# Padding so that the tiles TensorE reads begin on a multiple of 128 bytes in SBUF

## The chip, the cores and the metric

The kernel runs on one core of a Trainium2 chip. The metric is the device time of one execution in microseconds (us). Lower is better. The on-chip memory from which the engines read is SBUF: 128 partitions, each a row of bytes. A tile is a block of bytes at the same address in every partition, and "address" below always means the byte address inside a partition. TensorE (PE in the profile) reads two tiles for each matmul: the stationary one (the weights, loaded ahead by a weight load, PEld) and the moving one, which it streams past the weights. VectorE is DVE, ScalarE is ACT.

## The reference

One layer of an encoder for 1024 tokens of width 1024, all in float32:

```python
h = x + 0.5 * swiglu_ffn(rmsnorm(x, norm_ffn1), ffn1_w_in, ffn1_w_out)      # D_FF = 2816
proj = rmsnorm(h, norm_mix) @ w_in                                         # q, k, v, g_ret, p, gates
ret = rmsnorm_per_head(retention(rotary(q), rotary(k) / 16, v)) * silu(g_ret)
pool_out = multiscale_pool(p, pool_w, pool_scale)
gate = sigmoid(gates + gate_bias)
merged = gate[0] * (ret @ w_ret_up) + gate[1] * (pool_out @ w_pool_up)
h = h + merged @ w_out
h = h + 0.5 * swiglu_ffn(rmsnorm(h, norm_ffn2), ffn2_w_in, ffn2_w_out)
out = rmsnorm(h, norm_final)
```

## The kernel before, in words

Every large product is done in three matmuls with float32r operands (`mm3`, lines 171 to 173): each operand tile holds a high part and a low part side by side, written by ACT (`copy`, L151) and DVE (`tt`, L152) in `split`, and the product is high x high + high x low + low x high. Most products are 128x128 weights against 512 moving columns. In the common parts of pairs of groups (`common`) and in the retention stage they have 256 moving columns. The seven-product scheme in `strassen`, `pairs_of_both` and `ffn_out` makes further operand tiles from sums and differences, which is DVE's work.

The stages run one after the other: the first feed-forward block's input products (names `a_...`), its output products (`b...`), the projections, retention with pooling, the merge, and the second feed-forward block (`c_...`, `d...`). `Flow` sets the order: each step prepares its weights four steps ahead, and between steps one or two pieces of deferred DVE and ACT work are issued. The order of instructions is fixed when the program is built.

**Where tiles lie.** Tiles come from two pools in SBUF, `cp` (constants, kept throughout) and behind it `sb`. In a pool, each tag has its own buffers, tags follow each other in the order of their first use, and each buffer takes its size, rounded up to 32 bytes. The tiles of `cp` take 256 (`vec`), 256 (`neg`), 1344 (`cst`), 32 (`warm`), 1024 (`zero`) and 512 (`ones_r`) bytes, from address 1152 on, so `sb` begins at 4576, which is 96 bytes past a multiple of 128. In `sb` the order is: 13 buffers of 4096 bytes (tags `t4`, nine, and `raw`, four); the two buffers of `ss`, of 32 bytes each (sums of squares, eight columns, tiles `x_sums`, `ss0` to `ss3` and `n4sse`); 37 buffers of 4096 bytes (tags `mv`, `wt`, `tl`); eight of 2048 (`c2`); then small tiles and `dec`. All slices that matmuls take of a tile begin at multiples of 512 bytes from its start, so the remainder of an address by 128 is that of its tile.

Worked out from the built program's addresses, the 10668 matmuls of the kernel before divide as follows. The offsets are those of the moving and of the stationary tile, in bytes past a multiple of 128.

| moving columns | moving at | stationary at | matmuls | what they are |
|---|---|---|---|---|
| 512 | 32 | 32 | 8028 | nearly all products |
| 512 | 32 | 96 | 14 | `ones_r` as weights |
| 256 | 32 | 32 | 1818 | `common`, retention |
| 256 | 32 | 96 | 144 | retention, weights `sm` (a `t4` buffer) |
| 256 | 96 | 32 | 372 | blocks and `state` kept in `t4` buffers |
| 128 | 32 | 32 | 96 | scores of retention |
| 128 (transposes) | 0 | 32 or 96 | 144 | moving is the identity in `cst` |
| 1 and idle (`zero`) | 0 or 96 | 96 | 52 | token sums, the start |

Of the kernel before, what the change touches and what calls it, by code (L numbers as in the profile page):

```python
# [10 lines left out]
F32 = mybir.dt.float32  # L11
# [6 lines left out]
P = 128  # L18
# [71 lines left out]
def block_kernel(ctx: ExitStack, tc, x, x_tok, vecs, f1_in, f1_out, w_in, w_v, pool_w, w_ret, w_pool, w_o,  # L90
# [10 lines left out]
    cp = ctx.enter_context(tc.tile_pool(name="cp", bufs=1))  # L101
    sb = ctx.enter_context(tc.tile_pool(name="sb", bufs=1))
# [14 lines left out]
    def tl(name):  # L117
        return sb.tile([P, S], F32, tag="tl", bufs=N_TL, name=name)
# [4 lines left out]
    def c2(name):  # L123
        return sb.tile([P, H], F32, tag="c2", bufs=N_C2, name=name)

    def bank(name):
        return ps.tile([P, H], F32, tag="ps", name=name)

    def sum_bank(name):

        return ps.tile([P, H], F32, tag="sum", bufs=N_SUM, name=name)

    def load(dst, src):
        nc.sync.dma_start(dst, src)
# [4 lines left out]
    def half(t, j):  # L139
        return t[:, j * H : (j + 1) * H]  # L140
# [52 lines left out]
            mm(b, zero[:, :P], zero, start=True, stop=True)  # L193
    ident, ones = cst[:, C_ID : C_ID + P], cst[:, C_ONE : C_ONE + P]
    ones_r = cp.tile([P, P], F32R, name="ones_r")


    def inverse_root(sums, n, name):
# [17 lines left out]
    def token_sums(ssq, tiles, name):  # L216

        sums = bank(f"{name}sum")
        for k, j in enumerate(tiles):
            mm(sums[:, k : k + 1], ssq[:, j * P : (j + 1) * P], ones[:, :1], start=k == 0, stop=True,  # L220
               skip_group_check=True)
        return sums[:, : len(tiles)]

    def spread(r, name):

        n = r.shape[-1]
        b = bank(f"{name}b")[:, : n * P]
        r2 = sb.tile([P, 2, 8], F32R, tag="r2", bufs=1, name=f"{name}r2")
        split(r2[:, 0, :n], r2[:, 1, :n], r)
        for z in range(2):  # L230
            dg = sb.tile([P, H], F32R, tag="c2", bufs=N_C2, name=f"{name}dg{z}")[:, : n * P]
            for j in range(n):
                at, by = dg[:, j * P : (j + 1) * P], r2[:, z, j : j + 1].bitcast(F32)
                if z:
                    nc.vector.tensor_scalar(at, ident, by, None, MUL)
                else:
                    act(at, ident, AF.Copy, scale=by)
            mm(b, ones_r, dg, start=not z, stop=bool(z))
        return b
# [175 lines left out]
    def strassen(nx, wa, wb, name, evac, end, begin=None, shared=(), dest=None):  # L415
# [43 lines left out]
        def b1():  # L459
            if begin:  # L460
                begin()
            t["a"] = bank(f"{name}a")
            prod("a", "L11", "R11", True, False)
            t["b"] = sum_bank(f"{name}b")
            with soon():
                copy(t["b"], t["a"])
# [535 lines left out]
    load(cst, consts)  # L1002
    flow.add(lambda: copy(ones_r, ones))
    first.work(first.r11, first.r21, first.r12, first.r22, first.p22, first.t2, first.t3, first.t1, first.t4_)
    x_sums = sb.tile([P, 8], F32, tag="ss", bufs=2, name="x_sums")

    def x_square(t):
        r = tl(f"xs{t}")
# [38 lines left out]
    def await_stored(*names):  # L1047
        flow.until(lambda: stored.issuperset(names))
# [311 lines left out]
    class Unit:  # L1360
# [5 lines left out]
        def loads(self):  # L1366
            await_stored(f"q{self.h}", f"k{self.h}", f"v{self.name}")
            at = slice(self.nh * H, (self.nh + 1) * H)
            self.src = {}
            r = self.src["v"] = tl(f"v{self.name}")  # L1370
            load(r, vs[self.h // 2 * 2 + self.nh][:, self.h % 2 * S : (self.h % 2 + 1) * S])
            for n, spilled in (("q", qs), ("k", ks)):
                r = self.src[n] = tl(f"{n}{self.name}")
                for i in range(2):
                    load(half(r, i), spilled[2 * self.h + i][:, at])
            if self.nh == 0:
                self.dec = sb.tile([P, H], F32, tag="dec", bufs=1, name=f"dec{self.h}")
                load(self.dec, decay[self.h])
                self.ss = sb.tile([P, 8], F32, tag="ss", bufs=2, name=f"ss{self.h}")
                self.O = {}  # L1380

        def follow(self, u):
# [278 lines left out]
    class Last(Norm):  # L1661
# [15 lines left out]
        def turned(self, acc):  # L1677


            def gains():  # L1680
                self.row = sb.tile([P, S], F32, tag="mv", bufs=N_MV, name=f"{self.name}row")
                load(self.row, g_row)
                self.ssq_e = sb.tile([P, 8], F32, tag="ss", bufs=2, name=f"{self.name}sse")

            def done(n):

                o = self.rows[n] = sb.tile([P, S], F32, tag="mv", bufs=N_MV, name=f"{self.name}o{n}")
                b = self.turn([acc[mt] for mt in range(4)], n)
                act(half(o, 1), b, AF.Square, accum_out=self.ssq_e[:, n : n + 1])
                tt(half(o, 0), b, half(self.row, 0), MUL)  # L1690
                v = self.sums[n] = sb.tile([P, 8], F32, tag="st", bufs=10, name=f"{self.name}e{n}")[:, :1]
                nc.vector.tensor_scalar(v, self.ssq_e[:, n : n + 1], 1.0 / D, EPS, MUL, ADD)

            def rest(n):

                b = self.turn([acc[mt] for mt in range(4, 8)], n)
                if n < N_SUM:
                    self.banks[n] = sum_bank(f"{self.name}s{n}")
                    copy(self.banks[n], b)
                else:  # L1700
                    copy(half(self.rows[n], 1), b)

            return gains, *(lambda f=f, n=n: f(n) for n in range(4) for f in (done, rest))
# [144 lines left out]
```

## Time and profile before

| | |
|---|---|
| time, median of 3 runs | 2164.43 us (2164.16 to 2165.67) |
| profiled execution: span from first to last instruction | 2160.9 us (no other time is given for it; the median lies 3.5 us above) |
| PE busy | 2148.0 us (99%), 10668 matmuls |
| PEld busy | 1816.9 us (84%) |
| DVE busy | 1870.0 us (87%) |
| ACT busy | 1088.9 us (50%) |
| granted TensorE clock | 0.999 |
| DMA | 320.92 MB, 149 GB/s over the span |

The busy time of PE is a union of spans that overlap, since matmuls are pipelined: a matmul is shown as 0.39 us long where the next begins after 0.23 us. What a matmul costs in a dense run is therefore read from the distance of starts in the timeline, and not from its own length.

### The profile page before, as it was taken

What the parts mean: (1) busy time and instruction counts of PE and PEld (TensorE: products, weight loads), DVE (VectorE), ACT (ScalarE), POOL (GpSimd) and SP (SyncE); (2) the same over time, 40 slices, a digit from 0 to 9 for tenths busy, and PEclk for the clock granted to TensorE, in tenths of its full rate; (3) what the DMA queues carried; (4) which work ended last, traced back from release to release, by engine and by line L of the source; (5) the groups of instructions that cost most, each with busy time, mean ns of one, the idle gap of its engine ahead of it and who ended that gap; (6) DMA issues with size and microseconds to landing.
All of it is one profiled execution on the core that took longest, in us unless ns stands there. A gap on an engine that the chain in (4) does not pass through costs nothing.

```text
span 2160.9 us, 29697 instructions
## 1 busy us (share of the span) xinstructions
PE 2148.0 (99%) x10668; PEld 1816.9 (84%) x10668; DVE 1870.0 (87%) x3300; ACT 1088.9 (50%) x2047; POOL 0.2 (0%) x4
## 2 busy tenths in 40 slices
PE   9999999999999999999999999999999999999998
PEld 7888888888888888888888898887888888888887
DVE  8799899998788798899767877899999989999784
ACT  8544444545656444444426754446644444455463
POOL 0000000000000000000000000000000000000000
PEclk9999999999999999999999999999999999999999
DMA  7232323596323333333485567624133232359532
GB/s 261 69 129 104 101 93 127 165 339 207 122 93 107 109 127 108 118 107 119 153 268 191 167 224 256 218 97 160 65 117 103 98 107 99 118 185 334 178 122 78
DMA packets 117828, 320.92 MB, mean 149 GB/s; under 512 B 12976, under 2 KB 17200, under 8 KB 117680
## 3 DMA queue, kind: packets, MB, share of 16 engines
q1 hardware_dynamic: 117104, 317.97, 43.4%
q8 instruction: 83, 1.36, 0.3%
q10 hardware_dynamic: 576, 1.05, 0.1%
q14 instruction: 65, 0.53, 0.1%
HBM read 228.27 MB, written 90.70 MB: 148 GB/s over the span
## 4 chain that ended last, share of the span: by engine, by line
PE 90%; DVE 7%; ACT 1%; issue 1%; DMA 1%; SPq 0%; ACTq 0%; DVEq 0%
PE c_b L171 2%; PE c_b L173 2%; PE c_b L172 2%; PE a_b L173 2%; PE a_b L171 2%; PE a_b L172 2%; PE c_e L173 2%; PE c_e L171 2%; PE c_e L172 2%; PE a_e L173 2%; PE a_e L171 1%; PE a_e L172 1%; PE bp6b L172 1%; PE bp6b L173 1%; PE bp6b L171 1%; PE c_a L172 1%
## 5 line engine op out<-in xcount | busy, mean ns | idle before, releaser
L172 PE MATMUL c_b<-n3T,c_wS 128*128 128x512 f32 x176 | 68.5, 389 | 0.0
L173 PE MATMUL c_b<-n3T,c_wS 128*128 128x512 f32 x176 | 68.5, 389 | 0.0
L171 PE MATMUL c_b<-n3T,c_wS 128*128 128x512 f32 x176 | 68.2, 390 | 0.0
L171 PE MATMUL a_b<-n1T,a_wS 128*128 128x512 f32 x168 | 65.5, 390 | 0.0
L172 PE MATMUL a_b<-n1T,a_wS 128*128 128x512 f32 x168 | 65.4, 389 | 0.0
L173 PE MATMUL a_b<-n1T,a_wS 128*128 128x512 f32 x168 | 65.4, 389 | 0.0
L173 PE MATMUL a_a<-n1R,a_wL 128*128 128x512 f32 x120 | 46.7, 390 | 0.8 <-DVE a_wL L152 0.8
L171 PE MATMUL a_a<-n1R,a_wL 128*128 128x512 f32 x120 | 46.8, 390 | 0.0
L172 PE MATMUL a_a<-n1R,a_wL 128*128 128x512 f32 x120 | 46.7, 389 | 0.0
L172 PE MATMUL c_a<-n3R,c_wL 128*128 128x512 f32 x112 | 43.7, 390 | 0.0
L171 PE MATMUL c_a<-n3R,c_wL 128*128 128x512 f32 x112 | 43.6, 389 | 0.0
L173 PE MATMUL c_a<-n3R,c_wL 128*128 128x512 f32 x112 | 43.6, 389 | 0.0
L173 PEld LDWEIGHTS c_b<-n3T,c_wS 128*128 128x128 f32 x176 | 33.0, 188 | 6.9
L171 PEld LDWEIGHTS c_b<-n3T,c_wS 128*128 128x128 f32 x176 | 33.0, 188 | 6.9
L172 PEld LDWEIGHTS c_b<-n3T,c_wS 128*128 128x128 f32 x176 | 33.0, 188 | 6.8
L171 PEld LDWEIGHTS a_b<-n1T,a_wS 128*128 128x128 f32 x168 | 31.5, 188 | 6.8 <-ACT a_v L471 0.3
L173 PEld LDWEIGHTS a_b<-n1T,a_wS 128*128 128x128 f32 x168 | 31.5, 188 | 6.6
L172 PEld LDWEIGHTS a_b<-n1T,a_wS 128*128 128x128 f32 x168 | 31.5, 188 | 6.5
L173 PE MATMUL c_e<-n3T,c_wS 128*128 128x512 f32 x88 | 35.1, 399 | 0.4 <-DVE c_wS L152 0.4
L171 PE MATMUL c_e<-n3T,c_wS 128*128 128x512 f32 x88 | 34.5, 393 | 0.0
L172 PE MATMUL c_e<-n3T,c_wS 128*128 128x512 f32 x88 | 34.4, 391 | 0.0
L173 PE MATMUL a_e<-n1T,a_wS 128*128 128x512 f32 x84 | 33.4, 398 | 0.9 <-DVE a_wS L152 0.9
(3058 smaller groups left out, 8076.2 us busy)
## 6 DMA issues: line engine op xcount, KB each, us to landing
c_ra<-in_f_in SPq DMA_DIRECT2D x22, 512.0 KB, 3.6
c_rb<-in_f_in SPq DMA_DIRECT2D x22, 512.0 KB, 4.1
a_ra<-in_f_in SPq DMA_DIRECT2D x21, 512.0 KB, 3.6
a_rb<-in_f_in SPq DMA_DIRECT2D x21, 512.0 KB, 4.4
t<-au SPq DMA_DIRECT2D x11, 512.0 KB, 2.6
b<-ag SPq DMA_DIRECT2D x11, 512.0 KB, 2.7
r<-au SPq DMA_DIRECT2D x11, 512.0 KB, 3.6
br<-r SPq DMA_DIRECT2D x11, 512.0 KB, 5.4
```

What stands on the lines that cost most here:

```text
L171: mm(dst, w[0], m[0], start=start, stop=False, skip_group_check=True)
L172: mm(dst, w[0], m[1], start=False, stop=False, skip_group_check=True)
L173: mm(dst, w[1], m[0], start=False, stop=stop, skip_group_check=True)
```

## The change

It adds padding at two places and nothing else. A tile of 32 bytes that nobody uses, `line`, is put behind `ones_r` in `cp`. And the buffers of tag `ss` take 64 bytes in place of 32, of which the first eight columns are used, through a new helper `eights`.

```diff
+    def eights(name):
+
+        return sb.tile([P, 16], F32, tag="ss", bufs=2, name=name)[:, :8]
...
     ones_r = cp.tile([P, P], F32R, name="ones_r")
+    cp.tile([P, 8], F32, name="line")
...
-    x_sums = sb.tile([P, 8], F32, tag="ss", bufs=2, name="x_sums")
+    x_sums = eights("x_sums")
...
-                self.ss = sb.tile([P, 8], F32, tag="ss", bufs=2, name=f"ss{self.h}")
+                self.ss = eights(f"ss{self.h}")
...
-                self.ssq_e = sb.tile([P, 8], F32, tag="ss", bufs=2, name=f"{self.name}sse")
+                self.ssq_e = eights(f"{self.name}sse")
```

On each engine the instructions, their operands' names and shapes, their order, their semaphore waits and the queues of their DMAs stay as they were; only addresses move (and the row length of the `ss` tiles). In the built programs:

| tiles | address before | past 128 | address after | past 128 |
|---|---|---|---|---|
| `t4`, `raw` (13 of 4096 bytes) | 4576 and on | 96 | 4608 and on | 0 |
| `ss` (2) | 57824 and on | 96, 0 | 57856 and on | 0, 64 |
| `mv`, `wt`, `tl` (37 of 4096 bytes) | 57888 and on | 32 | 57984 and on | 0 |
| `c2` (8 of 2048 bytes) | 209440 and on | 32 | 209536 and on | 0 |
| `dec` (read by DVE alone) | 226432 | 0 | 226528 | 96 |
| `cst` (identity, column of ones) | 1664 | 0 | 1664 | 0 |
| `zero`, `ones_r` | 3040, 4064 | 96 | 3040, 4064 | 96 |

So all matmuls of the first table but those with `zero` or `ones_r` have both operands at a multiple of 128 afterwards.

## The prediction

> **What bounds the kernel now.** I read the page first, then the chain that ended last, the waits of PE, and the timeline of PE at places where operands lie differently. From the page, the span, the busy times and the granted clock:
>
> ```profile
> span 2160.9 us, 29697 instructions
> ...
> PE 2148.0 (99%) x10668; PEld 1816.9 (84%) x10668; DVE 1870.0 (87%) x3300; ACT 1088.9 (50%) x2047; POOL 0.2 (0%) x4
> ...
> PEclk9999999999999999999999999999999999999999
> ...
> PE 90%; DVE 7%; ACT 1%; issue 1%; DMA 1%; SPq 0%; ACTq 0%; DVEq 0%
> ```
>
> PE is busy for 2148.0 of 2160.9 us at the full clock, and the chain that ended last is PE for 90%. What PE waits for at all, from the waits of PE between 108 and 2000 us (line, releaser, us in total, times, longest):
>
> ```profile
> PE a_e L173 <- DVE a_wS L152: 0.9, 2, 0.5
> PE a_a L173 <- DVE a_wL L152: 0.8, 1, 0.8
> ```
>
> These two are the largest of that list, so there is next to no waiting to remove. Time can only change through what a matmul itself costs, or through a new wait. The cost of a matmul is the distance of starts. A dense run of 512 columns with both operands at 32 (timeline of PE: start, length, line, tiles):
>
> ```profile
> 599.71 0.39 PE L171 MATMUL bp5a<-bp3m,bp3w 128*128 128x512 f32 x1
> ...
> 603.79 0.39 PE L171 MATMUL bp5a<-bp3m,bp3w 128*128 128x512 f32 x1
> ```
>
> From the first to the last are 18 steps (19 rows, one after the other): 4.08 / 18 = 226.7 ns each. The page's 10668 matmuls are 8028 such (front table), so 8028 x 226.7 ns = 1820 us of the span.
>
> Now two pairs of runs that differ in a start address alone. First, in retention, the same moving tile `v` (at 32) against weights `kd` (at 32) and then against weights `sm` (at 96), all with 256 columns:
>
> ```profile
> 1182.22 0.28 PE L171 MATMUL st<-v,kd 128*128 128x256 f32 x1
> ...
> 1183.66 0.28 PE L171 MATMUL ob<-v,sm 128*128 128x256 f32 x1
> ...
> 1185.70 0.28 PE L171 MATMUL xb<-state,q 128*128 128x256 f32 x1
> ```
>
> Twelve steps in 1.44 us are 120.0 ns; eighteen in 2.04 us are 113.3 ns. Second, in the first feed-forward block, the same product with the moving block in a `tl` buffer (at 32) and 2 us later in a `t4` buffer (at 96), weights at 32 in both:
>
> ```profile
> 157.57 0.28 PE L171 MATMUL a_x<-n1R22y,a_ws 128*128 128x256 f32 x1
> ...
> 158.29 0.28 PE L171 MATMUL a_b<-n1R,a_ws 128*128 128x256 f32 x1
> ...
> 159.71 0.28 PE L171 MATMUL a_x<-n1R22y,a_ws 128*128 128x256 f32 x1
> ...
> 160.39 0.39 PE L171 MATMUL a_e<-n1T,a_wL 128*128 128x512 f32 x1
> ```
>
> Six steps in 0.72 us are 120.0 ns; six in 0.68 us are 113.3 ns. So the start address shows in PE's pace, on the moving and on the stationary side alike. The size of it: 512 columns cost 226.7 ns and 256 cost 120.0 at the same offsets, so 256 more columns cost 106.7 ns, 0.417 ns a column. What is left over beside the columns is 226.7 - 213.3 = 13.3 ns, and 120.0 - 106.7 = 13.3 ns: the same for both widths, once per matmul, 32 columns' worth. In the other two runs it is 6.7 ns, 16 columns or 64 bytes of a float32 row. A surplus in whole steps of 64 bytes, once per matmul, that depends on where the operands begin is what reading a row in pieces would give, when a row that begins inside a piece touches one piece more.
>
> **The change part by part.** It adds no instruction and no wait and moves none past another, so its whole effect lies in addresses.
>
> *Matmuls with both operands at 32.* The trace before has no dense run with both at 0. From above, the surplus that stays is 6.7 ns, that of the better runs; from below it is nothing, the bare columns. I take the middle, 3.3 ns, as neither end is nearer to a row, so 10.0 ns are saved each: 8028 x 10.0 = 80.3 us and 1818 x 10.0 = 18.2 us. At the ends, 9846 x 6.7 = 65.6 us and 9846 x 13.3 = 131.3 us.
>
> [...]
>
> *The 516 matmuls of 256 columns with one operand at 96.* Their surplus is 6.7 ns now; between nothing and all of it goes, 3.3 ns: 1.7 us (0 to 3.4). All other matmuls (transposes, 128 wide, token sums) are 306, and 1 ns on each is 0.3 us: nothing.
>
> Sum on PE: 80.3 + 18.2 + 1.7 = 100.2 us, between 65.6 and 134.7.
>
> *DVE and ACT.* They read the same tiles at new addresses. Their present offsets differ too, and DVE shows nothing of it: operands in `c2` and `wt` (32) against operands in `t4` (96), the groups by form, count, busy us, mean ns:
>
> ```profile
> L152 DVE TENSOR_TENSOR c_wS<-c_S,c_wS 128x512 fp32r<-128x512 f32 x46 | 31.4, 685 | 1.2 <-ACT c_wS L151 1.2
> ...
> L716 DVE TENSOR_TENSOR cu<-cu,n3rb 128x512 f32<-128x512 f32 x44 | 30.1, 685 | 0.0
> ```
>
> Both 685 ns. I count nothing for them, and nothing for DMA, whose transfers are hidden by prefetch; if either did get slower, the next part says where it would show.
>
> *What is late next.* PE's busy share covers everything else; where DVE is nearly as busy, a faster PE uncovers it. The windows of the two feed-forward input stages, the long middle, and two stretches of heavy DMA inside the first two (us of window, PE, PEld, DVE, ACT, POOL busy, clock, DMA share, GB/s):
>
> ```profile
> 108.00:486.00 378.00, 375.57 (x1939) 319.84 (x1938) 355.19 (x640) 178.23 (x328) 0.00 (x0) 1.00 0.44 151
> 1458.00:1998.00 540.00, 538.53 (x2730) 457.97 (x2729) 511.28 (x916) 278.87 (x513) 0.00 (x0) 1.00 0.40 138
> ...
> 486.00:1458.00 972.00, 970.93 (x4841) 824.58 (x4839) 804.63 (x1390) 481.73 (x932) 0.00 (x0) 1.00 0.47 155
> ...
> 432.00:486.00 54.00, 54.00 (x240) 44.72 (x239) 51.45 (x86) 26.16 (x48) 0.00 (x0) 1.00 0.95 339
> 1944.00:1998.00 54.00, 54.00 (x240) 44.69 (x239) 51.52 (x86) 27.36 (x50) 0.00 (x0) 1.00 0.94 332
> ```
>
> In the middle DVE is busy for 83%: the gain comes through. In the two feed-forward stages (918 us, 4669 of 10668 matmuls, so 44% of the saving, 44 us) DVE has 918 - 866.5 = 51.5 us of idle time. What of that can close? Its waits for PE go when PE is faster; the largest in each stage:
>
> ```profile
> DVE au L710 <- PE a_b L173: 8.6, 10, 1.1
> ...
> DVE cu L710 <- PE c_b L173: 12.3, 14, 1.1
> ```
>
> That is 20.9 us; the rest are waits for ACT and DMA, which a faster PE does not shorten. So I take 21 us of the 44 as had and 23 as given back in new waits of PE on DVE (`a_wL`, `a_wS`, `c_wL`, `c_wS`). Two windows of 54 us with DMA at 0.95 and 0.94 lie in the same stages: the transfers there could hold PE as well, and are in the 23.
>
> Sum: 100.2 - 23 = 77 us off the span of 2160.9, 2083.9 us; with the 3.5 us by which the median of the runs lies above the span, **2087 us**. Ends: 134.7 us on PE, of which 59 in these stages against at most 51.5 us of idle time, is 127 us, 2037; but that needs no DVE wait left at all, and with 21 us had there it is 97 us, 2068. I draw the lower end between them, at 2050. The smallest saving, 65.6 us with 29 in these stages and 21 had, is 57 us: 2107.
>
> **The rivals.** *The offset to each other counts, not the offset itself* (no change). In the slow runs the two operands have equal remainders, in the quicker ones they differ by 64. Afterwards all are equal again. Then 8028 and 1818 stay as they are and the 516 lose their advantage: 516 x 6.7 = 3.4 us more, 2168 us. For it: both pairs of runs fit it as well as they fit the pieces. Against: the surplus would be 13.3 ns from any equal start, which the trace can't show. [...] Chance 0.21, of which 0.17 within 0.2%.
>
> *Both streams now begin a piece at the same instant and collide* (slower). PE starts a matmul and the load of the next weights together; with both rows cut at the same places, each matmul could pay one more step of 6.7 ns than now: 9846 x 6.7 = 66 us and 516 x 13.3 = 7 us, 2237 us. It decides as soon as the dense run stands above 226.7 ns: 0.1 ns on 9846 matmuls is 1 us, which with the 3.4 us passes 0.2% (4.3 us, about what a measurement of this kernel can tell from no change). For it: equal remainders are the slow case today. Against: a start inside a piece is the only thing in the trace that explains a whole step. Chance 0.11.
>
> *DVE gives it all back.* PE gets faster by 100 us, but in the feed-forward stages DVE's idle time is needed as it is, for its chain with ACT: 44 us are lost, 56 stay, 2108 us. Chance 0.08. That the padding misses its aim is no rival: the addresses of the built program, in the table above, are at 0.
>
> **How the numbers follow.** The forecast, fewer pieces per row, has 0.57; the rest of 0.03 is a mixture (one side gains alone), faster for 0.02 and within 0.2% for 0.01. Faster: 0.57 + 0.08 + 0.02 = 0.67. Within 0.2%: 0.17 + 0.01 = 0.18. Slower: 0.04 + 0.11 = 0.15. The likeliest case's own range is 2050 to 2107. The range for 8 in 10 must reach the rival of no change, whose 2168 I round up to 2169; it leaves out the collision and the tails, 0.15 or so.
>
> **What would show it.** In the profile after: the dense run `bp5a` at 213 to 220 ns between starts, `st` and `ob` at one and the same pace of 107 to 113 ns; DVE's 685 ns unchanged; DVE busy above 96% in the two feed-forward stages, and PE waits on `a_wL`, `a_wS`, `c_wL` and `c_wS` that sum to some 23 us in place of 2. Wrong if the dense run stays at 226.7 ns (then the rival of equal offsets, with `ob` at 120), or rises; wrong in size if PE's pace falls and its waits are far from 23 us.

## The result and the profile after

The changed kernel took 2165.92 us (median of 12 runs, 2163.38 to 2166.49) and the kernel before 2164.63 us (12 runs beside it, 2162.61 to 2166.25). The ratio is 1.0005, 95% interval 0.9996 to 1.0013: no change that can be measured, where the forecast was 2087 us. The medians differ by 1.3 us, while the runs of either kernel scatter by more than 3. The page of the profile after (span; busy times of the engines; granted clock; the chain that ended last by engine):

```profile
span 2163.9 us, 29697 instructions
...
PE 2150.2 (99%) x10668; PEld 1818.9 (84%) x10668; DVE 1869.6 (86%) x3300; ACT 1089.2 (50%) x2047; POOL 0.2 (0%) x4
...
PEclk9999999999999999999999999999999999999999
...
PE 93%; DVE 5%; ACT 1%; issue 1%; DMA 0%; SPq 0%; ACTq 0%; DVEq 0%
```

PE is busy for 2150.2 us instead of 2148.0, over the same 10668 matmuls at a granted clock of 0.999, as before. Its idle time is 13.7 us (2163.9 - 2150.2), where it was 12.9. The two largest waits of PE between 108 and 2000 us (line, releaser, us in total, times, longest):

```profile
PE a_x L175 <- DVE ag L568: 1.2, 1, 1.2
PE a_e L177 <- DVE a_wS L156: 0.9, 2, 0.5
```

None of the waits that a faster PE would have met is there, because PE is not faster. The timeline of PE, first in the dense run of 512 columns (start, length, line, tiles; 18 steps lie between the two rows):

```profile
599.79 0.39 PE L176 MATMUL bp5a<-bp3m,bp3w 128*128 128x512 f32 x1
...
603.87 0.39 PE L176 MATMUL bp5a<-bp3m,bp3w 128*128 128x512 f32 x1
```

4.08 us / 18 = 226.7 ns, the pace of before to the digit, although both operands now begin at a multiple of 128. The same timeline in retention, weights `kd` (12 steps from the first row to the second), then weights `sm` (18 steps from the third row to the fourth):

```profile
1182.72 0.28 PE L175 MATMUL st<-v,kd 128*128 128x256 f32 x1
...
1184.16 0.28 PE L175 MATMUL st<-v,kd 128*128 128x256 f32 x1
...
1185.60 0.28 PE L175 MATMUL ob<-v,sm 128*128 128x256 f32 x1
...
1187.73 0.28 PE L175 MATMUL xb<-state,q 128*128 128x256 f32 x1
```

`st` stays at 1.44 / 12 = 120.0 ns. `ob` has lost its advantage: 2.13 / 18 = 118.3 ns, where it was 113.3. So has the block in a `t4` buffer (six steps from the second row to the third):

```profile
158.41 0.28 PE L175 MATMUL a_x<-n1R22y,a_ws 128*128 128x256 f32 x1
...
160.56 0.28 PE L175 MATMUL a_x<-n1R22y,a_ws 128*128 128x256 f32 x1
...
161.27 0.40 PE L175 MATMUL a_e<-n1T,a_wL 128*128 128x512 f32 x1
```

0.71 / 6 = 118.3 ns, before 113.3. The three stages by windows (us of window; PE, PEld, DVE, ACT, POOL busy; clock; DMA share; GB/s):

```profile
108.00:486.00 378.00, 374.82 (x1935) 319.42 (x1933) 353.57 (x637) 176.23 (x326) 0.00 (x0) 1.00 0.43 149
486.00:1458.00 972.00, 971.26 (x4838) 825.32 (x4837) 804.11 (x1390) 483.63 (x934) 0.00 (x0) 1.00 0.47 156
1458.00:1998.00 540.00, 538.53 (x2727) 457.95 (x2726) 510.77 (x915) 276.47 (x507) 0.00 (x0) 1.00 0.40 137
```

Each window holds three or four matmuls fewer than before (1935, 4838, 2727 for 1939, 4841, 2730), ten in all, some 2 us of matmuls; no stage stands out. DVE's two groups, by form:

```profile
L156 DVE TENSOR_TENSOR c_wS<-c_S,c_wS 128x512 fp32r<-128x512 f32 x46 | 31.3, 681 | 1.2 <-ACT c_wS L155 1.2
...
L721 DVE TENSOR_TENSOR cu<-cu,n3rb 128x512 f32<-128x512 f32 x44 | 29.9, 683 | 0.0
```

681 and 683 ns, where both were 685: DVE is no slower at the new addresses. ACT's busy time is 1089.2 us, before 1088.9.

**What did change.** The two profiled spans are 3.0 us apart (2163.9 and 2160.9). Two executions of one kernel can differ by as much (the 12 of the kernel before lie within 3.6 us), but what single matmuls cost can be read more closely. In what follows, the *distance* of a matmul is the start of its stationary tile minus the start of its moving tile, in bytes modulo 256. Before, `t4` lay at 224 and `mv`, `wt`, `tl`, `c2` at 32 modulo 256 (addresses of the front table); afterwards they lie at 0 and at 128. Grouping all matmuls of the two traces by columns and distance, with the time from each start to the next one (means without those over 110% of the median, totals with all):

| columns, distance | before: matmuls, ns, total us | after: matmuls, ns, total us |
|---|---|---|
| 512, 0 | 8027, 227.0, 1832.0 | 8027, 227.1, 1832.9 |
| 256, 0 | 1818, 119.7, 221.7 | 1818, 119.7, 221.2 |
| 256, 64 (moving in `t4`) | 372, 115.6, 44.9 | none |
| 256, 192 (weights `sm`) | 144, 113.4, 16.3 | none |
| 256, 128 | none | 516, 118.8, 63.9 |

The 516 cost 63.9 - 44.9 - 16.3 = 2.7 us more, waits included; by the mean paces alone it is 61.3 - 43.0 - 16.3 = 2.0 us. The other large groups are the same within 1 us.

### The profile page after: what moved, and what is told of

Read it like the earlier page. It is cut to its first block, busy times and chain, and to the rows that moved or that the text cites. A ratio compares the mean times of both kernels' runs of the same rounds, so it can differ in the third digit from the quotient of the medians.

```text
span 2163.9 us, 29697 instructions
## 1 busy us (share of the span) xinstructions
PE 2150.2 (99%) x10668; PEld 1818.9 (84%) x10668; DVE 1869.6 (86%) x3300; ACT 1089.2 (50%) x2047; POOL 0.2 (0%) x4
## 4 chain that ended last, share of the span: by engine, by line
PE 93%; DVE 5%; ACT 1%; issue 1%; DMA 0%; SPq 0%; ACTq 0%; DVEq 0%
PE c_b L175 2%; PE c_b L176 2%; PE c_b L177 2%; PE c_e L177 2%; PE a_b L177 2%; PE a_b L175 2%; PE a_b L176 2%; PE c_e L175 2%; PE c_e L176 2%; PE a_e L177 2%; PE a_e L176 1%; PE a_e L175 1%; PE c_a L176 1%; PE c_a L177 1%; PE c_a L175 1%; PE bp6b L176 1%
## 5 line engine op out<-in xcount | busy, mean ns | idle before, releaser
L177 PE MATMUL c_e<-n3T,c_wL 128*128 128x512 f32 x88 | 34.3, 390 | 0.0
```

The source lines that it names most:

```text
L177: mm(dst, w[1], m[0], start=False, stop=stop, skip_group_check=True)
```

## The experiments

Three theories stand in the expectations. "Relative": only the distance of the two starts counts. "Pieces", that of the prediction: each start counts by itself. "Fixed": 512 columns cost the same wherever they lie; that weight load and matmul are equally long at 256 columns, as its text has it, no trace shows (the trace before has them 188 and 276 ns long in `ob`). Edits are against the kernel before unless said otherwise.

**1. A scan of distances.** A kernel of matmuls alone, in groups of 30 with one PSUM bank each (the tile that takes the sums) and without a pause between them. It leaves the layer out. The last four numbers of a group are its moving columns, its weights' columns, the moving start and the stationary start in bytes.

```diff
+    for i in range(32):
+        out.append((f"wide_{letter(i)}", "r", 512, 128, 0, 32 * i))
+    for i in range(32):
+        out.append((f"half_{letter(i)}", "r", 256, 128, 0, 32 * i))
+    for i in range(16):
+        out.append((f"shifted_{letter(i)}", "r", 512, 128, 32, 32 * i))
...
+                nc.tensor.matmul(b[:wide, :cols], B[:, by : by + wide], A[:, at : at + cols], start=s == 0,
```

> A program of matmuls alone, which computes nothing of the reference: 119 groups of 30 float32r or bf16 matmuls with the other engines at rest, the moving tile held at one start and the weights' start stepped by 32 bytes (groups wide_a, wide_b, ... : 512 columns, weights 0, 32, 64 ... 992 bytes past the moving start modulo 1024; half_*: the same with 256 columns; shifted_*: moving at 32; fine_*: weights stepped by 4 bytes; mid_*: 384 columns, steps of 64; narrow_* and thin_*: weights of 64 and of 32 columns, steps of 64; bf_*: bf16, steps of 64). Theory 'relative' (the distance between the two starts sets the surplus): at distance 0 the pace is 226.7 ns with 512 columns and 120.0 with 256; at 64 and at 192 modulo 256 it is 220.0 and 113.3; at 128 about 225 and 118.7, as the runs of the changed kernel with unequal tiles show; shifted_b (both at 32) is as wide_a (both at 0). Theory 'pieces' (each start by itself, the prediction's): wide_a and half_a are the quickest and any weights' start off a multiple of 64 costs 6.7 ns. Theory 'fixed' (512 columns always cost 226.7, and distance shows only where weight load and matmul are equally long, at 256 columns): wide_* all 226.7, half_* 113.3 to 120. If two read streams collide, narrow_* and thin_* at distance 0 have a smaller surplus than 13.3 ns, about a half and a quarter of it; if it is a cost per matmul, they stay at 226.7.

In the timeline of PE a row is a group here, so the pace is the distance of two rows' starts by 30 (the step from one group into the next included):

```profile
25.44 6.97 PE L61 MATMUL wide_a<-moving,weight 128*128 128x512 f32 x30
32.25 7.15 PE L61 MATMUL wide_b<-moving,weight 128*128 128x512 f32 x30
39.24 7.16 PE L61 MATMUL wide_c<-moving,weight 128*128 128x512 f32 x30
...
255.38 3.57 PE L61 MATMUL half_c<-moving,weight 128*128 128x256 f32 x30
258.78 3.77 PE L61 MATMUL half_d<-moving,weight 128*128 128x256 f32 x30
...
361.75 7.16 PE L61 MATMUL shifted_a<-moving,weight 128*128 128x512 f32 x30
368.75 6.97 PE L61 MATMUL shifted_b<-moving,weight 128*128 128x512 f32 x30
375.56 7.15 PE L61 MATMUL shifted_c<-moving,weight 128*128 128x512 f32 x30
...
626.10 6.65 PE L61 MATMUL bf_a<-movingb,weightb 128*128 128x512 bf16 x30
632.58 6.64 PE L61 MATMUL bf_b<-movingb,weightb 128*128 128x512 bf16 x30
639.06 6.64 PE L61 MATMUL bf_c<-movingb,weightb 128*128 128x512 bf16 x30
```

`wide_a` (both starts at 0) runs at 6.81 / 30 = 227.0 ns and `wide_b` (0 and 32) at 6.99 / 30 = 233.0. With the moving tile at 32, the weights at 0 (`shifted_a`) give 7.00 / 30 = 233.3 and the weights at 32 (`shifted_b`) 6.81 / 30 = 227.0. So the distance counts and neither start by itself, and the surplus of some 13 ns is there from starts at 0 as well. Inside the groups, behind their first steps, all distances:

| distance, bytes | 0 | 32 | 64 | 96 | 128 | 160 | 192 | 224 |
|---|---|---|---|---|---|---|---|---|
| 512 columns, ns | 226.7 | 233.3 | 233.3 | 234.2 | 232.4 | 233.3 | 228.9 | 233.3 |
| 256 columns, ns | 120.0 | 118.3 | 113.3 | 120.0 | 118.5 | 120.0 | 117.8 | 117.8 |

(At 128 the steps repeat in a rhythm of seven, whose mean is 232.4 ns; the 232.8 of later expectations is a mean over part of it.) From 256 bytes on the row repeats, to the tenth of a nanosecond in nearly all of 32 steps. "Pieces" and "fixed" fall, and "relative" is right that the distance decides; but the 220.0 ns that it gave 512 columns at 64 and 192 was wrong (233.3 and 228.9). The two widths want different distances: 512 columns are quickest at 0, where 256 have 120.0 ns, the slowest of the table, and 256 are quickest at 64, where 512 have 233.3. Nor is distance all: at 192 the kernel before ran its 144 matmuls with `sm` at 113.4 ns, where this scan has 117.8. Experiments 6 and 7 take that up. The part of the expectation on narrower weights missed: with 64 weight columns the four distances 0, 64, 128, 192 gave 230.0, 232.7, 229.4 and 228.3 ns, with 32 columns 231.0 to 231.7. At distance 0 the surplus does not shrink with the bytes that the weight load reads; it grows (226.7, 230.0, 231.7 ns). In bf16 the pace is 6.48 / 30 = 216.0 ns, at each of the eight multiples of 64 that were tried. The float32r groups with 512 columns, whose best is 226.7 ns, came no nearer to that at any address tried here.

**2. One half of the change: `line` alone.** All starts move by 32 bytes, so `mv`, `wt`, `tl` lie at 64 and `t4` at 0 modulo 256: every start is a multiple of 64, and the distances are those of before.

```diff
     ones_r = cp.tile([P, P], F32R, name="ones_r")
+    cp.tile([P, 8], F32, name="line")
```

> The first half of the change alone: the pad behind ones_r, with the ss buffers as before. t4 and raw buffers lie at 0 modulo 256, mv, wt, tl and c2 at 64, so the distance between the two kinds is 64 again as before (192 modulo 256 one way, 64 the other), while both starts are multiples of 64. Theory 'relative': dense 512 at 226.7 ns, retention's st at 120.0 and ob at 113.3, the y blocks in t4 buffers at 113.3, as before; time 2161 to 2166 us, some 2 us below the changed kernel's on PE. Theory 'pieces' with pieces of 64 bytes: all runs at their quickest, dense 512 at 213 to 220, time 2060 to 2110.

One run took 2162.74 us, the kernel before beside it 2162.63. The timeline of PE at the block in `t4` (six steps):

```profile
159.91 0.28 PE L171 MATMUL a_x<-n1R22y,a_ws 128*128 128x256 f32 x1
...
160.59 0.39 PE L171 MATMUL a_e<-n1T,a_wL 128*128 128x512 f32 x1
```

0.68 / 6 = 113.3 ns: the advantage of before is kept. Over the whole trace the 512-column matmuls average 227.0 ns, the others at distance 0 119.7, at 64 115.7, at 192 113.4. New offsets at old distances change nothing.

**3. The other half: the `ss` tiles alone.** Here `mv`, `wt`, `tl` lie at 96 past a multiple of 128 and so does `t4`; the distance between the two kinds is 128, as after the change.

```diff
-    x_sums = sb.tile([P, 8], F32, tag="ss", bufs=2, name="x_sums")
+    x_sums = eights("x_sums")
```

> The second half of the change alone: ss buffers of 64 bytes, without the pad behind ones_r. All large tiles lie at 96 past a multiple of 128; modulo 256 mv, wt, tl and c2 at 96, t4 and raw at 224, so the distance between the kinds is 128 as in the changed kernel. Theory 'relative': everything as in the changed kernel: dense 512 at 226.7 ns, ob about 118.7, time within 2 us of it, 2163 to 2168 us. Theory 'pieces': a surplus of 3 to 13 ns that differs from the changed kernel's, and ob equal to st.

One run took 2165.49 us. At the same place of the timeline:

```profile
159.76 0.28 PE L175 MATMUL a_x<-n1R22y,a_ws 128*128 128x256 f32 x1
...
160.47 0.40 PE L175 MATMUL a_e<-n1T,a_wL 128*128 128x512 f32 x1
```

0.71 / 6 = 118.3 ns, and the 516 average 118.7: as in the changed kernel, with no large tile at a multiple of 128. Experiments 2 and 3 split the change: what the 516 lost comes from the 32 bytes between the two kinds of tiles, and the line of 128 does nothing. The two times are single runs and could not show this; the paces do.

**4. A fine scan, and which meeting counts.** Distances in steps of 4 bytes over 256, and groups in which two distances alternate. The layer is left out.

```diff
+    for i in range(64):
+        out.append((f"wide_{letter(i)}", 512, (0,), (4 * i,)))
+    for i in range(64):
+        out.append((f"half_{letter(i)}", 256, (0,), (4 * i,)))
+    for i, d in enumerate((64, 128, 192)):
+        out.append((f"own_{letter(i)}", 512, (0, d), (0, d)))
+        out.append((f"next_{letter(i)}", 512, (0, d), (d, 0)))
```

> Matmuls alone again, which compute nothing of the reference. wide_* and half_*: 512 and 256 columns, float32r, the distance from the moving to the weights' start stepped by 4 bytes over the whole period of 256 (aa is 0, ac 8, ca 64, ea 128, ga 192). Theory 'relative': wide_aa 226.7 ns and no distance quicker; half_ca 113.3 and no distance quicker; every other distance between. If a quicker distance for 512 columns exists, it shows here. own_* and next_*: the starts of successive matmuls alternate between 0 and d (64, 128, 192). In own_* each matmul's weights lie at its own moving start, so the weights that are loaded beside it lie d off; in next_* its own weights lie d off and those loaded beside it at distance 0. If it is the load beside the matmul that meets it, next_* keep 226.7 (512 columns) and own_* cost what wide_* cost at d (233.3, 232.8, 228.9); if it is the pair that is multiplied, the other way round. cols_aa to cols_ad: 512, 448, 320 and 288 columns at distance 0: 13.3 ns over 0.4167 ns a column in each, if the surplus is once per matmul: 226.7, 200.0, 146.7, 133.3.

Nothing lies below 226.7 ns with 512 columns. Besides 0, seven other distances reach it (120, 132, 144, 156, 204, 228, 252); the slowest, 164, gives 237.4 (steps of 230, 229, 234, 257 and 237 ns in turn). With 256 columns the range is 113.3 (at 52, 64, 76, 88 and 180) to 123.3 (at 204). Four bytes change the pace by several nanoseconds (`wide_aa`, distance 0, 5.45 / 24 = 227.1 and `wide_ab`, distance 4, 5.58 / 24 = 232.5, the step into the next group included), so no line size shows to which one could align. At distance 128 this scan has 233.5 ns in a rhythm of two steps (238 and 229), where experiment 1 had 232.4 in one of seven. The surplus is not the same at every width: 320 columns run at 146.7 ns, as forecast, but 448 at 202.7 (forecast 200.0) and 288 at 131.8 (forecast 133.3). The alternating groups (24 matmuls; 128 bytes is the pair that alternates here):

```profile
577.64 5.65 PE L54 MATMUL own_ab<-moving,weight 128*128 128x512 f32 x24
583.12 5.68 PE L54 MATMUL next_ab<-moving,weight 128*128 128x512 f32 x24
588.64 2.99 PE L54 MATMUL ownhalf_ab<-moving,weight 128*128 128x256 f32 x24
```

5.48 / 24 = 228.3 and 5.52 / 24 = 230.0 ns. Neither the constant distance 0 to a matmul's own weights nor that to the next ones keeps 226.7, and the pairs with 64 and 192 don't either (231.6 to 233.3). Inconclusive; experiment 9 takes it up.

**5. Distance 64 for most of the layer.** The whole layer, both edits of the change (the lines shown are against the changed kernel), and 192 bytes of unused tile ahead of the `mv` buffers: 7560 of the 512-column matmuls get distance 64, 336 get 192, and 1722 of the 256-column ones get 64.

```diff
     def mv(name):
+        if not gap:
+            gap.append(sb.tile([P, 48], F32, tag="gap", bufs=1, name="gap"))
         return sb.tile([P, 2, H], F32R, tag="mv", bufs=N_MV, name=name)
```

> The changed kernel with one unused tile of 192 bytes between the wt buffers and the mv buffers: same instructions, waits and order, and nearly all matmuls (7560 of 512 columns, 1722 of 256) have their weights at distance 64 modulo 256 from the moving tile, in place of 0. Theory 'relative', with the scan's paces: dense 512 at 233.3 ns in place of 226.7, 7560 x 6.7 = +50 us; 256 columns at 113.3 in place of 120, 1722 x 6.7 = -11 us; sum +39 us on PE, time 2200 to 2208 us, ratio 1.017 to 1.020. Theory 'fixed' (512 columns cost 226.7 wherever they lie): no slower than the kernel before, 2155 to 2166 us. Theory 'pieces' (each start by itself): both tiles at multiples of 64 as in the changed kernel, no change.

2205.50 us, ratio 1.019 (1.0176 to 1.0203). The page's engine row, and from the timeline of PE the dense run (18 steps):

```profile
PE 2188.9 (99%) x10668; PEld 1812.8 (82%) x10668; DVE 1876.3 (85%) x3300; ACT 1088.7 (49%) x2047; POOL 0.2 (0%) x4
```

```profile
602.01 0.39 PE L181 MATMUL bp5a<-bp3m,bp3w 128*128 128x512 f32 x1
...
606.21 0.39 PE L181 MATMUL bp5a<-bp3m,bp3w 128*128 128x512 f32 x1
```

4.20 / 18 = 233.3 ns, the scan's figure for distance 64. The sum: 7560 x (233.3 - 227.0) = 47.6 us, 336 x (228.9 - 227.0) = 0.6, 1722 x (115.2 - 119.7) = -7.7, together 40.5; PE's busy time grew by 2188.9 - 2148.0 = 40.9. "Fixed" and "pieces", which forecast no slowdown here, fall in the layer too. Addresses can move this kernel by 1.9%, and the padding left 9846 of 10668 matmuls at distance 0, where they had been.

**6. Each width at its own distance.** If 512 columns want 0 and 256 want 64, the 256-column `common` parts can get weights that begin 64 bytes on, with all other large tiles at distance 0 (the lines shown are against the changed kernel; the same edit for the weights `x`, `s34` and `y`, and the two moves for space that the expectation names):

```diff
-    def wt(name):
-        return sb.tile([P, 2, 4, P], F32R, tag="wt", bufs=N_WT, name=name)
+    def wt(name, shift=0):
+        t = sb.tile([P, 1088], F32R, tag="wt", bufs=N_WT, name=name)
+        return t[:, shift : shift + 1024].rearrange("p (j a b) -> p j a b", j=2, a=4)
...
-            w["s12"] = weights(s, f"{A.name}ws12{n}")
+            w["s12"] = weights(s, f"{A.name}ws12{n}", 16)
```

> A version meant to beat both: the changed kernel with wt buffers of 4352 bytes, in which the weights of the common products alone (all 1806 of their matmuls have 256 columns) begin 64 bytes later, the ss buffers padded to 128 bytes so that all other large tiles are at distance 0 modulo 256, and the zero tile moved into a c2 buffer for the space. Same instructions, waits and order. Theory 'relative': 512 columns stay at 226.7 ns; the common products go from 120 (some 118) to 113.3, 1806 x 6 to 6.7 = 11 to 12 us less on PE than the changed kernel; retention's 528 are at 120. With up to a half given back in the feed-forward stages, where DVE is busy for 94%, 2154 to 2160 us, ratio to the kernel before 0.995 to 0.998. Theory 'fixed' for 256 columns or a cover by DVE throughout: ratio 0.999 to 1.001.

2163.18 us, ratio 0.9994 (0.9985 to 1.0003): not the gain expected. The page's engine row, and from the timeline of PE six matmuls of a common part:

```profile
PE 2147.2 (99%) x10668; PEld 1816.2 (84%) x10668; DVE 1868.9 (87%) x3300; ACT 1088.9 (50%) x2047; POOL 0.2 (0%) x4
```

```profile
157.26 0.28 PE L176 MATMUL a_x<-n1R22y,a_ws 128*128 128x256 f32 x1
...
157.97 0.28 PE L176 MATMUL a_b<-n1R,a_ws 128*128 128x256 f32 x1
```

0.71 / 6 = 118.3 ns here, 117.8 on average over 1806 matmuls at distance 64, where the scan had 113.3 and the kernel before 115.6. PE is busy for 3.0 us less than in the changed kernel, where 11 to 12 were forecast. One distance has two paces. In the scan the run at 64 was entered from a group at 32; here it is entered from 512 columns.

**7. What decides between the two paces.** Matmuls alone; runs of 36 with 256 columns at distance 64, each entered from another run.

```diff
+    for rep in range(3):
+        for lead, cols, d, steps in (("wide", 512, 0, 24), ("six", 256, 0, 6), ("long", 256, 0, 24), ("one", 256, 0, 1),
+                                     ("two", 256, 0, 2), ("three", 256, 0, 3), ("far", 512, 192, 24), ("mid", 384, 0, 24)):
+            out.append((f"base_{letter(n)}", 512, (0,), (0,), 24))
+            out.append((f"{lead}_{letter(n)}", cols, (0,), (d,), steps))
+            out.append((f"{lead}then_{letter(n)}", 256, (0,), (64,), 36))
```

> Matmuls alone, float32r, the layer left out. Runs of 36 matmuls with 256 columns at distance 64, each entered from another run without a pause: from 24 of 512 columns at distance 0 or 192, from 24 of 384 at distance 0, and from 1, 2, 3, 6 or 24 of 256 at distance 0; each three times. 'Entry': the pace at distance 64 is one of two, 113.3 or 117.8 ns, and the run before decides: 117.8 after 512 columns, 113.3 after 6 or more of 256 at distance 0, and some count between 1 and 6 where it turns; the three repeats agree. 'Chance or content': the pace is not set by the run before: the repeats of one case differ, or all cases have one pace (113.3, as in the scan, or 117.8). Four runs of 36 at distance 0 serve as the scale: 119.8 to 120.0 ns.

The timeline by groups, for three ways in; each run of 36 ends where the next `base` starts:

```profile
33.68 4.40 PE L56 MATMUL widethen_aa<-moving,weight 128*128 128x256 f32 x36
37.92 5.63 PE L56 MATMUL base_ab<-moving,weight 128*128 128x512 f32 x24
...
66.50 4.24 PE L56 MATMUL onethen_ad<-moving,weight 128*128 128x256 f32 x36
70.58 5.63 PE L56 MATMUL base_ae<-moving,weight 128*128 128x512 f32 x24
...
76.28 4.40 PE L56 MATMUL twothen_ae<-moving,weight 128*128 128x256 f32 x36
80.52 5.63 PE L56 MATMUL base_af<-moving,weight 128*128 128x512 f32 x24
```

After 512 columns 4.24 / 36 = 117.8 ns; after a single matmul of 256 columns at distance 0, 4.08 / 36 = 113.3; after two of them 117.8 again. So also after 3, 6 and 24, after 384 columns, and after 512 at distance 192. All three repeats of each case agree, and a run keeps the pace that it entered with for all of its 36. The entry decides, as "entry" said; but the rule that it gave, 113.3 after six or more at 120 ns, is wrong.

The kernel before had both paces too, in one and the same product: `xb` (moving tile `state`, distance 64), in the timeline of PE behind `ob` (first two rows) and behind `st` (last two), from the fourth of its twelve matmuls on:

```profile
1186.06 0.28 PE L171 MATMUL xb<-state,q 128*128 128x256 f32 x1
...
1187.12 0.39 PE L171 MATMUL px<-pl,pw 128*128 128x512 f32 x1
...
1203.07 0.28 PE L171 MATMUL xb<-state,q 128*128 128x256 f32 x1
...
1204.09 0.28 PE L171 MATMUL ob<-v,sm 128*128 128x256 f32 x1
```

Nine steps in 1.06 us are 117.8 ns, nine in 1.02 us are 113.3. All four `xb` behind `st` have 113.3; of the eight behind `ob` six have 117.8, and the two with a longer step (741 and 170 ns) among their first have 113.3. But `st` is a run of 256 columns at distance 0, behind which the matmuls alone took 117.8. In the layer the moving start goes from 32 to 224 there and the weights' stays; in the matmuls alone the weights' start moves and the other stays. Whether that is the difference, no run shows.

**8. The same in the layer.** Experiment 6 with the weights `wx` left at distance 0. Its expectation was written without the result of experiment 7. It takes the matmuls with `wx` for the first six of 21; in the timeline they are the first and the third six of the 42 of a common part, 516 of 1806 in all, so runs at 0 and at 64 alternate at first.

```diff
-            w["x"] = weights(a[src], f"{A.name}wx{n}", 16)
+            w["x"] = weights(a[src], f"{A.name}wx{n}")
```

> The whole layer at equal offsets as in the version with all weights of `common` 64 bytes on, but with the weights `wx` of each common part left at distance 0: its first 6 matmuls run at distance 0, the 15 behind them (1290 in all, with those of the second kind) at 64. 'Entry': the 6 settle at 120 ns and the run then goes on at about 121, 121, 116 and 113.3 ns from there, a mean near 114.5 over the 15, where that version had 117.8; 1290 x (119.7 - 114.5) = 6.7 us off PE against equal offsets, ratio 0.996 to 0.999. 'Chance or content': the 15 stay at 117.8 as before, 1290 x 1.9 = 2.5 us off, ratio 0.9985 to 1.0003.

2163.88 us, ratio 0.9998 (0.9989 to 1.0007). The other 1290 average 117.9 ns, which is what experiment 7 gives behind six matmuls at distance 0; that kernel's engine row:

```profile
PE 2149.9 (99%) x10668; PEld 1817.8 (84%) x10668; DVE 1869.7 (86%) x3300; ACT 1091.3 (50%) x2047; POOL 0.2 (0%) x4
```

The time is that of the second theory's line, though its name is wrong: the pace is not chance, but the six were the wrong entry. The 113.3 ns that the expectation had behind such a run were read from the kernel before, where the moving start changes and not the weights'. A common part entered by a single matmul at distance 0, which had 113.3 in experiment 7, is not among the runs. No version here beats the kernel before by more than a measurement can tell.

**9. Own weights or next weights, with both distances free.** Matmuls alone, 512 columns; both starts step on together, so that the distance to a matmul's own weights and to the next ones are chosen apart.

```diff
+                at = (step * s) % 256 // 4 + 512 * (s % 2)
+                by = (own + step * s) % 256 // 4 + 128 * (s % 4)
```

> Matmuls alone, float32r, the layer left out. Groups of 24 matmuls with 512 columns in which both starts step on by a fixed number of bytes each time, so that the distance of a matmul's weights to its own moving tile (first letter of the group's name, in steps of 32 bytes: a is 0, c is 64, e is 128, g is 192) and the distance of the weights loaded next to the moving tile then being read (second letter) are each constant and chosen freely: all 64 pairs. Scale from the first scan: 226.7 ns at distance 0, 233.3 at 64, 232.8 at 128, 228.9 at 192. 'Next': the load of the next weights meets the moving tile being read: the pace goes by the second letter alone; all groups with second letter a at 226.7, all with c at 233.3. 'Own': by the first letter alone; all groups with first letter a at 226.7. 'Rhythm': it is neither meeting, but the regular step from one instruction's start to the next: only the eight groups with both letters alike (no step) keep the scan's paces, and the others lie between, 228 to 235, by no single letter.

```profile
23.41 5.60 PE L51 MATMUL own_aa<-moving,weight 128*128 128x512 f32 x24
28.85 5.78 PE L51 MATMUL own_ab<-moving,weight 128*128 128x512 f32 x24
...
112.18 5.75 PE L51 MATMUL own_ca<-moving,weight 128*128 128x512 f32 x24
117.77 5.75 PE L51 MATMUL own_cb<-moving,weight 128*128 128x512 f32 x24
```

`own_aa`, with no step, has 5.44 / 24 = 226.7 ns; `own_ca`, with the next weights at distance 0 and its own at 64, 5.59 / 24 = 232.9. Inside the groups, at multiples of 64:

| own distance | next 0 | next 64 | next 128 | next 192 |
|---|---|---|---|---|
| 0 | 226.7 | 228.3 | 228.5 | 231.7 |
| 64 | 232.8 | 233.3 | 228.3 | 229.9 |
| 128 | 230.0 | 233.9 | 233.3 | 232.4 |
| 192 | 231.6 | 230.0 | 231.7 | 228.9 |

Neither a row nor a column is constant. Of the 64 pairs only 0 with 0 has 226.7; of the eight without a step seven have the scan's figures within 0.2 ns, and distance 128 has 233.3 for 232.4. That is the picture of "rhythm", which is the weakest of the three, since it says only that no single meeting explains it.

## Why the prediction was wrong

- **The step that failed** is the reading of the surplus: "a row that begins inside a piece touches one piece more", each start by itself. From it came 80.3 us on 8028 matmuls and 18.2 us on 1818. Both were worth nothing: the dense run stayed at 226.7 ns and the 256-column runs at distance 0 at 119.7. The two pairs of runs that carried it changed an absolute offset and a distance together, as the rival of equal offsets said; the objection to that rival, a surplus of 13.3 ns "from any equal start", is what the scan found from 0 and from 32 (227.0 ns in both, with the step into the next group). Nor did those pairs "differ in a start address alone": they also stand behind different matmuls, which experiment 7 shows to count (113.3 or 117.8 ns).
- **The surplus as a count of steps.** 13.3 and 6.7 ns looked like whole steps of 64 bytes, the same at both widths. Steps of 4 bytes give many other sizes, 448 columns have a surplus of 16.0 ns and 288 one of 11.8, and 113.3 is only one of two paces at distance 64.
- **The 516 matmuls**: 1.7 us saved was forecast, 2.7 us more was measured, 2.0 of it in the mean paces. The rival gave 3.4, with 120.0 ns for all; they average 118.8.
- **The rival that happened** had 2168 us and a chance of 0.21; the median was 2165.92. The range ended at 2169 for this rival's sake; the forecast's own likeliest case ended at 2107, so that the time lies inside is no merit of the mechanism. The rival was still too simple in one point: equal remainders are the quickest case with 512 columns, not the slow one.
- **The collision** did not come from the change. A matmul and the load of the next weights do start together (trace before, `bp5a`: the matmul of L171 and the load of L172 both at 599.71 us), but it decided "as soon as the dense run stands above 226.7 ns", and it stands at it (4.08 / 18 again). What looks like it, 233.3 ns, belongs to distance 64 (experiment 5), so its reason against equal remainders was upside down.
- **DVE and ACT at nothing**: right (DVE 681 and 683 ns; ACT busy for 1089.2 us, before 1088.9). **What is late next**, 23 us of new waits, was never put to the test, as PE got no faster.
- **The weights' start** does count in float32r: with the moving tile at 0 it changes the pace by up to 10.7 ns (226.7 to 237.4, experiment 4). Whether it is the load of the next weights that takes this time, no run shows; experiment 9 found no pace that goes by the next weights' distance alone.

What stays open is the mechanism. It goes by the starts of both tiles (`shifted_a` 233.3 ns, `shifted_b` 227.0), has a period of 256 bytes (32 steps of experiment 1), is absent in bf16 at multiples of 64 (216.0 ns at all eight), does not shrink at distance 0 with narrower weights (226.7, 230.0, 231.7 ns), and a run of 256 columns at distance 64 keeps the pace that its entry gave it (113.3 or 117.8 ns over all 36); that is shown. What in the reading of the tiles produces it was not found.

## What to carry to other kernels

Two runs in a trace that differ in one address also differ in its distance to the other operand; before a padding is built on such a pair, a kernel of matmuls alone that moves both starts together (`shifted_b` here) tells the two readings apart. In float32r kernels, give the tiles of 512-column products starts that are equal modulo 256, the quickest distance found here (226.7 ns): distance 64 cost this kernel 1.9%, and a round address gave nothing (ratio 1.0005). A pace measured in one dense run needn't hold for the same instructions behind other ones (113.3 and 117.8 ns in experiment 7), so an estimate from it should carry the other pace as its second end.

## What the runs showed of the hardware

- The pace of float32r matmuls goes by the distance of the stationary to the moving start, modulo 256 bytes: 226.7 to 237.4 ns with 512 columns, 113.3 to 123.3 with 256 (experiment 4). In bf16 there is none of it at multiples of 64 (216.0 ns at eight distances).
- At distance 0 the surplus over 0.417 ns a column is 13.3 ns at 512 and at 256 columns (226.7, 120.0), and also at 320 (146.7); at 448 it is 16.0 (202.7) and at 288 11.8 (131.8).
- One and the same stream of matmuls (256 columns, distance 64) has two steady paces, 113.3 and 117.8 ns, and what ran just before it chooses. With 512 columns at distance 128 it was 232.4 in one scan and 233.5 in another.
